# Both ends of a two-layer encoder trunk: constant products and VectorE scaling first, kept weight splits and shared squares last

## The chip, the cores and the metric

The kernel runs on one core of one Trainium2 chip. The core has five engines, each with its own instruction queue that is worked in order: TensorE (PE, matrix products; PEld is its weight load), VectorE (DVE), ScalarE (ACT), GpSimd (POOL) and SyncE (SP), which here issues most of the DMA transfers. The metric is the device time of one execution in microseconds (us); lower is better.

## The reference

The input is one sequence of 1024 frames with 1024 channels. Layer 0 mixes along time with RWKV-7 (a recurrence with data-dependent decay), layer 1 with a diagonal complex state-space model; each mixer is followed by a squared-ReLU MLP, and every sub-layer ends in a layer norm. All data are float32. Cut to what the change touches, the first low-rank projections and the last MLP with its norm:

```python
def layer_norm(x, g, b):
    mu = jnp.mean(x, axis=-1, keepdims=True)
    var = jnp.mean(jnp.square(x - mu), axis=-1, keepdims=True)
    return (x - mu) * lax.rsqrt(var + LN_EPS) * g + b

def rwkv7_time_mix(x, mu, w0, w1, w2, a0, a1, a2, g1, g2, ...):
    xx = jnp.pad(x, ((0, 0), (1, 0), (0, 0)))[:, :-1] - x
    xw = x + xx * mu[1]
    xa = x + xx * mu[4]
    w_pre = w0 + jnp.tanh(xw @ w1) @ w2
    a = jax.nn.sigmoid(a0 + (xa @ a1) @ a2)
    ...

def sq_relu_mlp(x, w1, w2):
    return jnp.square(jax.nn.relu(x @ w1)) @ w2

def reference(x, ...):
    h = x
    for i in range(2):
        mix = rwkv7_time_mix(h, ...) if i == 0 else s5_mix(h, ...)
        h = layer_norm(ALPHA * h + mix, ln_g[2 * i], ln_b[2 * i])
        h = layer_norm(ALPHA * h + sq_relu_mlp(h, mlp_w1[i], mlp_w2[i]),
                       ln_g[2 * i + 1], ln_b[2 * i + 1])
    return h
```

## The kernel before

Everything is held transposed: a tile has 128 channels as partitions and frames along the row, so a 1024-channel activation of half the sequence (512 frames, "A" or "B") is eight tiles of 128x512. Products are made at near float32 precision from two reduced-precision parts: `split` (L154) writes the high part with a cast on ACT (L155) and the low part, the remainder, with a subtraction on DVE (L156), and `mm3` (L206) sums three products (high by high, high by low, low by high), recorded at L204. Weights come by DMA into `wraw` (two buffers); the parts go to `whi` and `wlo` (three buffers each). A `wraw` buffer is free again when its subtraction on DVE is done.

**The beginning.** `rwkv_proj(0)` loads the eight tiles of x (`xs`, L272) and, with the first of them, two halves of the weight `wa1` (`first`, L274). `shifted` (L339) makes two products with the same weights, scaled once by 1 - mu and once by mu; `scaled` (L324) scales each 128x512 piece of weights on GpSimd (L331, two instructions of 128x4x64 where two coefficients share a piece), splits it and multiplies. The x tiles themselves are split to `oS`.

**The end.** The MLP of layer 1 for half B runs in blocks: `up(b)` (ub) makes two 128x512 tiles of squared ReLU (L1000 Relu, L1001 Square, then split into `qbuf`), `down(b)` (db) multiplies them by four weight tiles of 256 output channels and adds each product (six matmuls in one PSUM tile `d`, of which there are three) into the residual tiles `hB` on DVE (L1017). The last two `down` blocks, b = 2 and 3, are held back until all `up` blocks are done and are then run twice, once for each 256 frames (c = 0 and c = 1; L1525 to L1531). In both rounds each of the eight weight tiles is loaded and split (`wload`, L176): 16 loads. After c = 0 the generator `last_norm` (L917) of the first 256 frames is started at low priority (`rank(LN8R)`), so it lies beside the products of c = 1; its last part is resumed after the sums of the second norm, with `inorder` keeping its scaling (L958) behind the last of these sums (`last`).

**last_norm**, for 256 frames: the sums over the eight tiles go to GpSimd (L927, L928), DVE (L929, L930) and a product with a matrix of 1/1024 (`pm`, L934); DVE subtracts the mean (L937), ACT squares (L939 for k = 0 and 1, L942 with two `sq` buffers for the rest); six additions gather the squares into two tiles, two of them on GpSimd (k in LNT), four on DVE (L943); four matmuls with one column give the variance in rows (`pq`, L947); DVE adds epsilon (L949), GpSimd raises to -1/2 (L950), ACT spreads it (L952), PE transposes it back (`pr`, L955); DVE multiplies (L958), ACT applies gain and bias (L964; GpSimd for k = 6, L962), and each tile goes out by itself (L965, 128 KB, 8 stores for each c).

**The order.** The order within each engine isn't written by hand. A scheduler makes it when the program is built, from priorities (`rank`) and from a modelled timeline, over the whole program. The order at one place thus depends on what it takes everything before to last.

Of the kernel before, what the change touches and what calls it, by code (L numbers as in the profile page):

```python
# [32 lines left out]
TB = 2  # L33
JB = 4
# [28 lines left out]
LNU = (6,)  # L63
# [10 lines left out]
def trunk(ctx, tc, A):  # L74
# [183 lines left out]
    def rwkv_proj(H):  # L258
# [65 lines left out]
        def scaled(nm, parts):  # L324
            p = psd()
            n = 128 // len(parts)
            for k0 in range(0, KT, 4):
                w = first.pop(0) if first else wraw(nm, k0)
                for q, m in enumerate(parts):
                    wq = w[:, :, q * n : q * n + n]  # L330
                    G.tensor_mul(wq, wq, m[:, k0 : k0 + 4].unsqueeze(2).broadcast_to([128, 4, n]))  # L331
                hi = wp.tile([128, 4, 128], F32R, tag="whi", name="whi")
                lo = wp.tile([128, 4, 128], F32R, tag="wlo", name="wlo")
                split(w, hi, lo)
                for k in range(4):
                    mm3(p, hi[:, k], lo[:, k], xo[k0 + k][0], xo[k0 + k][1], k0 + k == 0, k0 + k == KT - 1)
            return p
# [580 lines left out]
    def last_norm(h, gi, c):  # L918
# [8 lines left out]
        G.tensor_add(a, hc[0], hc[1])  # L927
        G.tensor_add(a, a, hc[2])  # L928
# [6 lines left out]
        sab = tp.tile([128, 2, HW], F32, tag="la", name="sq01", bufs=2)  # L935
        for k, t in enumerate(hc):
            V.tensor_sub(t, t, pm)  # L937
            if k < 2:
                S.activation(sab[:, k], t, AF.Square)  # L939
            else:  # L940
                q = tp.tile([128, HT], F32, tag="m", name="sq")[:, 0:HW]
                S.activation(q, t, AF.Square)  # L942
                last = (G if k in LNT else V).tensor_add(sab[:, int(k in LNT)], sab[:, int(k in LNT)], q)  # L943
        pq = bank.tile([128, HT], F32, tag=tag, name="pq")
        for t in range(2):
            for j in range(2):
                PE.matmul(pq[:, t : t + 1], sab[:, j, t * 128 : (t + 1) * 128], ones_c[:, 0:1], start=j == 0, stop=j == 1)  # L947
        rs = tp.tile([128, 4], F32, tag="rs", name="rs")[:, 0:2]
        V.tensor_scalar(rs, pq[:, 0:2], LN_EPS, None, op0=ALU.add)  # L949
# [6 lines left out]
        after = (yield last) if c == 0 else None  # L956
        for k, t in enumerate(hc):
            scaled = V.tensor_mul(t, t, pr[:, 0:HW])  # L958
            if after:
                inorder([after, scaled])  # L960
            if k in LNU:
                G.tensor_scalar(t, t, vec(g, k), vec(b, k), op0=ALU.mult, op1=ALU.add)  # L962
            else:
                S.activation(t, t, AF.Identity, bias=vec(b, k), scale=vec(g, k))  # L964
            SP.dma_start(A["out"][k * 128 : (k + 1) * 128, HT + HW * c : HT + HW * c + HW], t)  # L965
        yield last
# [22 lines left out]
    def blocks(i, h, xo, qbuf):  # L989
# [16 lines left out]
        def down(b, first=False, cs=slice(0, HT)):  # L1006
            for n2 in range(C // nw):
                w = wload(A["mw2"][i, b, n2], KB2, nw)
                for n in range(nw // 128):
                    p = psd()[:, cs]  # L1010
                    dense(p, [(x[:, n * 128 : (n + 1) * 128], y[:, n * 128 : (n + 1) * 128]) for x, y in w],
                          [(x[:, cs], y[:, cs]) for x, y in qs[b]])
                    z = h[n2 * (nw // 128) + n][:, cs]
                    if first:
                        V.scalar_tensor_tensor(z, z, ALPHA, p, op0=ALU.mult, op1=ALU.add)
                    else:
                        V.tensor_add(z, z, p)  # L1017
# [505 lines left out]
    for b in range(JB - TB + 1, JB):  # L1523
        ub(b)
    for c in range(2):  # L1525
        for b in range(JB - TB, JB):
            db(b, False, slice(256 * c, 256 * c + 256))
# [78 lines left out]
```

## Time and profile before

| | us |
|---|---|
| median of three runs | 2608.95 (2604.10 to 2617.72) |
| the profiled execution | 2612.68 |
| its span, from the first to the last instruction | 2610.9 |
| PE busy | 2475.1 (95%) |
| DVE busy | 1814.7 (70%) |
| ACT busy | 1205.8 (46%) |
| POOL busy | 411.9 (16%) |

The page of the profile divides the span into 40 slices of 65 us. PE is busy for 0.7 of the first slice, 0.8 to 0.9 or more from there to the last, and 0.7 of the last. Busy times of PE are modelled, since matmuls overlap; the start of one matmul to the start of the next tells more than the length of one. In a timeline row the columns are: start, length of the group, engine, line, operation, result<-operands, count, and in brackets how long the engine had been idle and what ended it. In a group's row the numbers behind the bar are busy us and mean ns of one instruction.

### The profile page before, as it was taken

Reading aid. Unit: us, or ns where it says so; the run is one execution under the profiler, and the core shown is the slowest. Engines: PE = TensorE matmul, PEld = TensorE weight load, DVE = VectorE, ACT = ScalarE, POOL = GpSimd, SP = SyncE. Lnnn points to the kernel's source line nnn. Section 1 sums busy time; section 2 is a strip of 40 time slices with the busy share of each in tenths; the row PEclk is TensorE's granted clock in tenths of the full one; section 3 lists DMA queues with packets and bytes.
Section 4 is the critical chain, followed back from the end, with each engine's and each line's share of the span. In section 5 each row is a group of like instructions: output and inputs, shape, how many; then the busy total and the mean of one; then the engine's idle time right before and its main releaser. Section 6 shows DMA issues by size and latency. Waiting matters only on the chain.

```text
span 2610.9 us, 43753 instructions
## 1 busy us (share of the span) xinstructions
PE 2475.1 (95%) x16624; PEld 2008.2 (77%) x16624; DVE 1814.7 (70%) x3476; ACT 1205.8 (46%) x2155; POOL 411.9 (16%) x340
## 2 busy tenths in 40 slices
PE   7889989999889999999999999999999999999997
PEld 5778767788667788777778888887777888888876
DVE  7477676578887777999785555777587555555576
ACT  7555575455454443445534333434464333433344
POOL 3110431331221101011000000100212111111011
PEclk9989979899889999999999999999999999999998
DMA  4765455555222324446554323254222111111123
GB/s 150 256 200 179 160 185 183 172 181 167 89 71 80 100 85 122 150 133 168 171 198 168 97 94 96 89 190 138 90 85 77 57 47 51 56 50 53 49 96 114
DMA packets 206291, 319.68 MB, mean 122 GB/s; under 512 B 20097, under 2 KB 80641, under 8 KB 206081
## 3 DMA queue, kind: packets, MB, share of 16 engines
q1 hardware_dynamic: 204928, 314.79, 38.4%
q8 instruction: 131, 2.15, 0.3%
q10 hardware_dynamic: 1152, 2.10, 0.2%
q14 instruction: 80, 0.65, 0.1%
HBM read 252.85 MB, written 63.96 MB: 121 GB/s over the span
## 4 chain that ended last, share of the span: by engine, by line
PE 70%; DVE 13%; DMA 8%; ACT 4%; issue 3%; POOL 1%; SPq 1%; ACTq 0%; DVEq 0%; POOLq 0%
PE d L204 52%; PE d L1054 9%; DVE wlo L156 2%; DMA wraw<-in_mw_dram 2%; PE pA L614 1%; DMA ldsg<-s_sg 1%; ACT whi L155 1%; PE pU L732 1%; PE pR L722 1%; DVE oAl L156 1%; PE pO L743 1%; PE pO L741 1%; DVE KB L584 1%; PE pX L727 0%; DMA s_y<-yg 0%
## 5 line engine op out<-in xcount | busy, mean ns | idle before, releaser
L155 ACT CAST whi<-wraw 128x512 fp32r<-128x512 f32 x492 | 304.6, 620 | 634.6 <-PE d L204 438.6
L156 DVE TENSOR_TENSOR wlo<-wraw,whi 128x512 fp32r<-128x512 f32 x492 | 356.3, 724 | 242.3 <-ACT whi L155 236.7
L204 PE MATMUL d<-qbuf,whi 128*128 128x512 f32 (+1 forms) x1344 | 410.0, 389 | 8.1 <-DVE hA L1017 4.5
L204 PE MATMUL d<-oAh,whi 128*128 128x512 f32 (+1 forms) x768 | 311.0, 411 | 17.1 <-ACT ev L435 7.3
L204 PE MATMUL d<-oAh,wlo 128*128 128x512 f32 (+1 forms) x768 | 310.9, 407 | 9.8 <-DVE wlo L156 7.8
L204 PE MATMUL d<-oAl,whi 128*128 128x512 f32 (+1 forms) x768 | 310.9, 406 | 3.1 <-DVE oAl L156 3.1
L204 PEld LDWEIGHTS d<-qbuf,whi 128*128 128x128 f32 x1344 | 246.4, 190 | 63.5 <-DVE hA L1017 8.4
L204 PE MATMUL d<-qbuf,wlo 128*128 128x512 f32 (+1 forms) x672 | 256.6, 385 | 1.5 <-DVE wlo L156 1.4
L204 PE MATMUL d<-oBh,wlo 128*128 128x512 f32 x512 | 202.7, 396 | 3.6 <-DVE wlo L156 3.6
L204 PE MATMUL d<-oBh,whi 128*128 128x512 f32 x512 | 203.0, 397 | 3.0 <-ACT whi L155 2.6
L204 PE MATMUL d<-oBl,whi 128*128 128x512 f32 x512 | 200.7, 392 | 0.0
L204 PEld LDWEIGHTS d<-oAh,whi 128*128 128x128 f32 (+1 forms) x768 | 147.7, 194 | 53.9 <-ACT ev L435 9.6
L204 PEld LDWEIGHTS d<-oAh,wlo 128*128 128x128 f32 (+1 forms) x768 | 149.0, 194 | 44.8 <-DVE wlo L156 10.4
L204 PEld LDWEIGHTS d<-oAl,whi 128*128 128x128 f32 (+1 forms) x768 | 148.5, 194 | 34.7 <-DVE oAl L156 4.1
L204 PE MATMUL d<-qh,wlo 128*128 128x512 f32 x384 | 151.3, 394 | 0.0
L204 PE MATMUL d<-ql,whi 128*128 128x512 f32 x384 | 150.6, 392 | 0.0
L204 PEld LDWEIGHTS d<-qbuf,wlo 128*128 128x128 f32 x672 | 127.1, 190 | 28.7 <-DVE wlo L156 3.1
L204 PE MATMUL d<-qh,whi 128*128 128x512 f32 x384 | 149.2, 389 | 0.0
L1017 DVE TENSOR_TENSOR hB<-hB,d 128x512 f32<-128x512 f32 (+1 forms) x168 | 104.9, 633 | 34.2 <-PE d L204 32.3
L204 PEld LDWEIGHTS d<-oBh,wlo 128*128 128x128 f32 x512 | 96.5, 189 | 27.8 <-DVE wlo L156 5.3
L1017 DVE TENSOR_TENSOR hA<-hA,d 128x512 f32<-128x512 f32 x144 | 97.5, 681 | 27.3 <-PE d L204 26.0
L204 PEld LDWEIGHTS d<-oBh,whi 128*128 128x128 f32 x512 | 96.5, 189 | 24.8 <-ACT whi L155 3.2
(478 smaller groups left out, 5079.2 us busy)
## 6 DMA issues: line engine op xcount, KB each, us to landing
wraw<-in_mw_dram SPq DMA_DIRECT2D x376, 256.0 KB, 2.7
wraw<-in_glu_dram SPq DMA_DIRECT2D x64, 256.0 KB, 2.7
low<-wlo SPq DMA_DIRECT2D x52, 256.0 KB, 2.8
wlo<-low SPq DMA_DIRECT2D x52, 256.0 KB, 3.3
raw<-in_mw_dram SPq DMA_DIRECT2D x48, 256.0 KB, 2.6
wraw<-in_wk_dram SPq DMA_DIRECT2D x32, 256.0 KB, 3.4
wraw<-in_wr_dram SPq DMA_DIRECT2D x32, 256.0 KB, 3.9
wraw<-in_wv_dram SPq DMA_DIRECT2D x32, 256.0 KB, 4.2
```

The source lines that it names most:

```text
L155: S.copy(hi, src)
L156: (e or V).tensor_sub(lo, src, hi.bitcast(F32))
L204: bulk.append((PE.matmul(p, w, x, **kw).ins, x.shape[-1]))
L584: V.scalar_tensor_tensor(kb[hs, :, h], v3(a)[hs], 0.5, v3(cs)[hs], op0=ALU.mult, op1=ALU.mult)
L614: prods.append(PE.matmul(pp[h][:, cc, i], D.KB[j][hs, u].rearrange("p j l -> p (j l)"), D.AR[j][hs, u].rearrange("p j l -> p (j l)"), star ...
L722: hop.append(PE.matmul(pR[hs, i], at[:, h, c, i, 0], vsa[:, cl, h, i], start=True, stop=True))
L732: hop.append(PE.matmul(pU[hs, i], D.kbt[i // 2, c // 2][:, c % 2, i % 2, hs], vsa[:, cl, h, i], start=True, stop=True))
L741: PE.matmul(pO[bs, i], arc(i, 1)[hs], st[hs, i], start=i == 0, stop=False, skip_group_check=True)
L743: PE.matmul(pO[bs, i], at[:, h, c, i, 1], vsa[:, cl, h, i], start=False, stop=True, skip_group_check=True)
L1017: V.tensor_add(z, z, p)
L1054: PE.matmul(p, w[:, k], x, start=not add and k + j == 0, stop=k == 3 and j == 2, skip_group_check=True)
```

## The change

There are four edits.

1. **Beginning.** For the very first piece of `wa1` (`begin`), ten products of the identity with itself (`WARM`) are put ahead of the real products, into the same PSUM tile, which the first real product overwrites; and the scaling of that one piece is done by DVE and not by GpSimd.
2. **Kept weights.** In the last two `down` blocks, run for c = 0 and c = 1, the parts of the weights are written to `jp` buffers (tags t1 and t2, eight of each, last used by the blocks before) and kept: c = 0 loads and splits eight tiles, c = 1 loads none.
3. **The last norm.** All eight squares have buffers of their own. For c = 0 the sums of squares go as before. For c = 1 three additions on DVE remain (k = 5, 6, 7 onto 4), and five tiles go to `pq`, ten matmuls where there were four. For c = 1 the first two sums (`sab`) go to DVE in place of GpSimd. The scaling of c = 0 is now held back in two parts: k up to 2 behind the last sum of squares of c = 1, the rest behind its epsilon (`steps`). Gain and bias: for c = 0 GpSimd does k = 1, 4, 6 (was 6); for c = 1 DVE does k = 2, 5 (GpSimd did 6); ACT does the others.
4. **Stores** go out for two tiles at a time, from new `pair` buffers: 256 KB, four for each c.

```diff
@@ -31,6 +31,7 @@
 LNG = (1, 3, 5)
 LNT = (2, 5)
 TB = 2
+WARM = 10
 JB = 4
 TABB = 6
 LN8R = 400000
@@ -60,7 +61,7 @@
 STE = "scalar"
 MIX0R = 1500
 EVB = 4
-LNU = (6,)
+LNU = ((1, 4, 6), (2, 5))
 VM = ((0, 1, 3), (1, 3))
 DECAY = math.exp(-0.5)
 ALPHA = math.sqrt(2.0)
@@ -325,10 +326,14 @@
             p = psd()
             n = 128 // len(parts)
             for k0 in range(0, KT, 4):
+                begin = len(first) == 2
+                if begin:
+                    for _ in range(WARM):
+                        PE.matmul(p[:, 0:128], ident, ident, start=True, stop=True)
                 w = first.pop(0) if first else wraw(nm, k0)
                 for q, m in enumerate(parts):
                     wq = w[:, :, q * n : q * n + n]
-                    G.tensor_mul(wq, wq, m[:, k0 : k0 + 4].unsqueeze(2).broadcast_to([128, 4, n]))
+                    (V if begin else G).tensor_mul(wq, wq, m[:, k0 : k0 + 4].unsqueeze(2).broadcast_to([128, 4, n]))
                 hi = wp.tile([128, 4, 128], F32R, tag="whi", name="whi")
                 lo = wp.tile([128, 4, 128], F32R, tag="wlo", name="wlo")
                 split(w, hi, lo)
@@ -924,46 +929,59 @@
         hc = [t[:, cs] for t in h]
         ab = tp.tile([128, 2, HW], F32, tag="la", name="sab", bufs=2)
         a, b2 = ab[:, 0], ab[:, 1]
-        G.tensor_add(a, hc[0], hc[1])
-        G.tensor_add(a, a, hc[2])
+        E = V if c else G
+        E.tensor_add(a, hc[0], hc[1])
+        E.tensor_add(a, a, hc[2])
         V.tensor_add(b2, hc[3], hc[4])
         V.tensor_add(b2, b2, hc[5])
         pm = bank.tile([128, HT], F32, tag=tag, name="pm")[:, 0:HW]
         parts = [a, b2, hc[6], hc[7]]
         for k, x in enumerate(parts):
             PE.matmul(pm, ones_c, x, start=k == 0, stop=k == 3)
-        sab = tp.tile([128, 2, HW], F32, tag="la", name="sq01", bufs=2)
+        sq = []
         for k, t in enumerate(hc):
             V.tensor_sub(t, t, pm)
-            if k < 2:
-                S.activation(sab[:, k], t, AF.Square)
-            else:
-                q = tp.tile([128, HT], F32, tag="m", name="sq")[:, 0:HW]
-                S.activation(q, t, AF.Square)
-                last = (G if k in LNT else V).tensor_add(sab[:, int(k in LNT)], sab[:, int(k in LNT)], q)
+            if k % 2 == 0:
+                q = tp.tile([128, 2, HW], F32, tag=("la", "m", "ev", "ev")[k // 2], name="sq", bufs=(2, 2, EVB, EVB)[k // 2])
+            sq.append(q[:, k % 2])
+            S.activation(sq[k], t, AF.Square)
+        if c == 0:
+            for k in range(2, KT):
+                last = (G if k in LNT else V).tensor_add(sq[int(k in LNT)], sq[int(k in LNT)], sq[k])
+            parts = sq[0:2]
+        else:
+            for k in range(5, KT):
+                last = V.tensor_add(sq[4], sq[4], sq[k])
+            parts = sq[0:5]
         pq = bank.tile([128, HT], F32, tag=tag, name="pq")
-        for t in range(2):
-            for j in range(2):
-                PE.matmul(pq[:, t : t + 1], sab[:, j, t * 128 : (t + 1) * 128], ones_c[:, 0:1], start=j == 0, stop=j == 1)
+        for j, x in enumerate(parts):
+            for t in range(2):
+                PE.matmul(pq[:, t : t + 1], x[:, t * 128 : (t + 1) * 128], ones_c[:, 0:1],
+                          start=j + t == 0, stop=j == len(parts) - 1, skip_group_check=True)
         rs = tp.tile([128, 4], F32, tag="rs", name="rs")[:, 0:2]
-        V.tensor_scalar(rs, pq[:, 0:2], LN_EPS, None, op0=ALU.add)
+        steps = last, V.tensor_scalar(rs, pq[:, 0:2], LN_EPS, None, op0=ALU.add)
         G.tensor_tensor(rs, rs, mhalf[:, 0:2], op=ALU.pow)
         rb = tp.tile([128, 4, 128], F32, tag="la", name="rb", bufs=2)
         S.copy(rb[:, 0:2], rs.unsqueeze(2).broadcast_to([128, 2, 128]))
         pr = bank.tile([128, HT], F32, tag=tag, name="pr")
         for j in range(2):
             PE.transpose(pr[:, j * 128 : (j + 1) * 128], rb[:, j], ident)
-        after = (yield last) if c == 0 else None
+        after = (yield steps) if c == 0 else None
         for k, t in enumerate(hc):
+            if k % 2 == 0:
+                pair = jp.tile([128, 2, HW], F32, tag=("qh", "ql")[c], name="pair", bufs=6)
             scaled = V.tensor_mul(t, t, pr[:, 0:HW])
             if after:
-                inorder([after, scaled])
-            if k in LNU:
-                G.tensor_scalar(t, t, vec(g, k), vec(b, k), op0=ALU.mult, op1=ALU.add)
+                inorder([after[int(k > 2)], scaled])
+            y = pair[:, k % 2]
+            if k in LNU[c]:
+                (V if c else G).tensor_scalar(y, t, vec(g, k), vec(b, k), op0=ALU.mult, op1=ALU.add)
             else:
-                S.activation(t, t, AF.Identity, bias=vec(b, k), scale=vec(g, k))
-            SP.dma_start(A["out"][k * 128 : (k + 1) * 128, HT + HW * c : HT + HW * c + HW], t)
-        yield last
+                S.activation(y, t, AF.Identity, bias=vec(b, k), scale=vec(g, k))
+            if k % 2:
+                SP.dma_start(A["out"][k * 128 - 128 : k * 128 + 128, HT + HW * c : HT + HW * c + HW]
+                             .rearrange("(k p) t -> p k t", p=128), pair)
+        yield steps
 
     def yload(H):
         ys = []
@@ -1003,9 +1021,22 @@
                 split(r, qt[:, 0], qt[:, 1])
                 qs[b].append((qt[:, 0], qt[:, 1]))
 
-        def down(b, first=False, cs=slice(0, HT)):
+        def kept(src):
+            raw = wp.tile([128, KB2, nw], F32, tag="wraw", name="wraw", bufs=2)
+            SP.dma_start(raw, src)
+            hi, lo = (jp.tile([128, HT], F32R, tag=t, name="k" + t, bufs=8).rearrange("p (k n) -> p k n", k=KB2)
+                      for t in ("t1", "t2"))
+            split(raw, hi, lo)
+            return [(hi[:, k], lo[:, k]) for k in range(KB2)]
+
+        def down(b, first=False, cs=slice(0, HT), keep=None):
             for n2 in range(C // nw):
-                w = wload(A["mw2"][i, b, n2], KB2, nw)
+                if keep is None:
+                    w = wload(A["mw2"][i, b, n2], KB2, nw)
+                else:
+                    if (b, n2) not in keep:
+                        keep[b, n2] = kept(A["mw2"][i, b, n2])
+                    w = keep[b, n2]
                 for n in range(nw // 128):
                     p = psd()[:, cs]
                     dense(p, [(x[:, n * 128 : (n + 1) * 128], y[:, n * 128 : (n + 1) * 128]) for x, y in w],
@@ -1522,9 +1553,10 @@
         db(b)
     for b in range(JB - TB + 1, JB):
         ub(b)
+    keep = {}
     for c in range(2):
         for b in range(JB - TB, JB):
-            db(b, False, slice(256 * c, 256 * c + 256))
+            db(b, False, slice(256 * c, 256 * c + 256), keep)
         if c == 0:
             with rank(LN8R):
                 early = last_norm(hB, 3, 0)
```

What the scheduler makes of it, at three places. In the rows of the change the line numbers are its own: L156 and L157 are the cast and the subtraction of `split`, L1018 and L1019 the Relu and Square of `up`, L1048 the addition into hB, L943 the subtraction of the mean, L954 the sums of squares, L973 the scaling, L962 the epsilon, L980 and L978 gain and bias.

ACT, from the last weight tiles of the last `up` to the last weight tile of the rounds c. Before (whi are casts of weights, the last 16 of them those of c = 0 and c = 1; rl and qbuf are Relu, Square and cast of the last `up`):

```order
L155 CAST whi<-wraw 128x512 x4
L1000 ACTIVATE rl<-d 128x512
L1001 ACTIVATE rl<-rl 128x512
L155 CAST qbuf<-rl 128x512
L155 CAST whi<-wraw 128x512 x2
L1000 ACTIVATE rl<-d 128x512
L1001 ACTIVATE rl<-rl 128x512
L155 CAST whi<-wraw 128x512
L155 CAST qbuf<-rl 128x512
L155 CAST whi<-wraw 128x512 x7
```

Now (the kt with a number are the high parts of the eight kept tiles, in order):

```order
L156 CAST kt_24879<-wraw 128x512
L1018 ACTIVATE rl<-d 128x512
L156 CAST kt_24901<-wraw 128x512
L1019 ACTIVATE rl<-rl 128x512
L156 CAST kt_24923<-wraw 128x512
L156 CAST qbuf<-rl 128x512
L156 CAST kt_24945<-wraw 128x512
L156 CAST kt_24967<-wraw 128x512
L1018 ACTIVATE rl<-d 128x512
L1019 ACTIVATE rl<-rl 128x512
L156 CAST qbuf<-rl 128x512
L156 CAST kt_24989<-wraw 128x512
```

Before the second Relu stood three casts of the rounds c; now five do, and the fifth is of the first tile of block 3.

DVE, from the last additions into hB to the end. Before:

```order
L1017 TENSOR_TENSOR hB<-hB,d 128x256
L937 TENSOR_TENSOR hB<-hB,pm 128x256 x8
L943 TENSOR_TENSOR sq_25281<-sq_25281,sq 128x256 x4
L958 TENSOR_TENSOR hB<-hB,pr 128x256 x8
L949 TENSOR_SCALAR rs<-pq 128x2
L958 TENSOR_TENSOR hB<-hB,pr 128x256 x8
```

Now:

```order
L1048 TENSOR_TENSOR hB<-hB,d 128x256
L943 TENSOR_TENSOR hB<-hB,pm 128x256 x8
L954 TENSOR_TENSOR sq<-sq 128x256 x3
L973 TENSOR_TENSOR hB<-hB,pr 128x256 x3
L962 TENSOR_SCALAR rs<-pq 128x2
L973 TENSOR_TENSOR hB<-hB,pr 128x256 x13
L978 TENSOR_SCALAR pair<-hB,pv 128x256 x2
```

Five of the eight scalings of c = 0 moved from ahead of the epsilon (rs) of c = 1 to behind it.

SP, in the recurrence of layer 0, where projections for half B are stored (s_a, s_sg) beside loads for the recurrence (ldsg, lda, ldk) and weights (wlo, wraw). Before:

```order
L531 DMA ldsg<-s_sg 128x2x256
L531 DMA lda<-s_a 128x2x256
L394 DMA s_a<-ev 128x512
L394 DMA s_sg<-ev 128x512
L394 DMA s_a<-ev 128x512
L531 DMA ldk<-s_k 128x2x256
L184 DMA wlo<-low_2363 128x512
L394 DMA s_sg<-ev 128x512
```

Now:

```order
L536 DMA ldsg<-s_sg 128x2x256
L536 DMA lda<-s_a 128x2x256
L536 DMA ldk<-s_k 128x2x256
L399 DMA s_a<-ev 128x512
L399 DMA s_sg<-ev 128x512 x2
L806 DMA s_y<-gt 128x4x128
```

No edit touches this place: the load of ldk moved ahead of three stores. Such exchanges run through the recurrence on all five engines. From the middle of the state-space layer to the last blocks of the last MLP the order on PE is unchanged.

## The prediction

> **What bounds the kernel now.** I read the table of stretches first, then the timeline of both ends, then their groups. In a row of stretches stand the stretch, its length, the busy us of PE, PEld, DVE, ACT and POOL, the granted clock and DMA.
>
> ```profile
> 200.00:400.00 200.00, 180.77 (x1840) 148.03 (x1838) 150.28 (x352) 119.65 (x227) 63.14 (x56) 0.90 0.54 174
> 400.00:600.00 200.00, 183.75 (x1837) 153.46 (x1836) 131.86 (x338) 107.24 (x203) 54.39 (x44) 0.93 0.60 182
> 600.00:800.00 200.00, 178.31 (x1755) 145.88 (x1755) 169.98 (x380) 98.56 (x185) 53.20 (x43) 0.90 0.31 97
> 100.00:800.00 700.00, 632.86 (x5990) 519.58 (x5989) 519.53 (x1191) 377.12 (x706) 188.64 (x159) 0.91 0.51 160
> 800.00:2560.00 1760.00, 1727.77 (x10082) 1399.31 (x10081) 1197.41 (x2081) 740.03 (x1289) 188.35 (x137) 0.99 0.33 104
> 2591.40:2611.00 19.60, 4.42 (x20) 3.37 (x18) 10.45 (x31) 10.41 (x23) 3.23 (x5) 0.66 0.32 107
> ```
>
> From 800 to 2560 us PE is busy for 98%: nothing the change does can shorten that. It can win in the first 20 us, in the two rounds of the last blocks (2560 to 2591) and in the norm behind them (2591 to 2611), where PE is idle for 15 of 19.6 us. And the new order can win or lose in 100 to 800, where PE stands idle for 700 - 632.9 = 67 us.
>
> **Kept weights.** First the rounds c, of which the timeline shows the start, the pitch and the end:
>
> ```profile
> 2559.97 0.40 PE L204 MATMUL d<-qbuf,whi 128*128 128x256 f32 x2
> 2560.21 0.28 PE L204 MATMUL d<-qbuf,wlo 128*128 128x256 f32 x1
> 2560.56 0.29 PE L204 MATMUL d<-qbuf,wlo 128*128 128x256 f32 x1
> 2586.60 0.95 PE L947 MATMUL pq<-ones_c,sq 128*128 128x1 f32 x8
> 2587.41 0.48 PE L204 MATMUL d<-qbuf,whi 128*128 128x256 f32 x2
> 2591.37 1.03 PE L934 MATMUL pm<-sab,ones_c 128*128 128x256 f32 x4
> 2592.24 1.03 PE L934 MATMUL pm<-hB,ones_c 128*128 128x256 f32 x4
> ```
>
> Three products take 0.355 us (2560.21 to 2560.56), one 0.119. The 16 weight tiles of 12 products need 192 x 0.119 = 22.8 us. Between them stands the first norm: pm 1.7 (eight records at 0.87 for four, 2591.37 to 2592.24), pq 0.8 (2586.60 to 2587.41), pr some 0.2 (two records of half the columns of pm). That makes 25.5 us, yet the rounds last 2591.37 - 2559.97 = 31.4: PE idles for 5.9. The cause is the supply of weights:
>
> ```profile
> 2568.19 0.62 ACT L155 CAST whi<-wraw 128x512 fp32r<-128x512 f32 x1 [1.39 <-DVE hB L1017]
> 2570.34 0.63 ACT L155 CAST whi<-wraw 128x512 fp32r<-128x512 f32 x1 [1.53 <-DMA wraw<-in_mw_dram]
> 2574.50 0.62 ACT L155 CAST whi<-wraw 128x512 fp32r<-128x512 f32 x1 [1.50 <-DMA wraw<-in_mw_dram]
> 2571.72 2.69 DMA wraw<-in_mw_dram
> L156 DVE TENSOR_TENSOR wlo<-wraw,whi 128x512 fp32r<-128x512 f32 x14 | 9.7, 694 | 5.3 <-ACT whi L155 5.2
> ```
>
> A freed wraw buffer costs 2.78 us until its next cast starts (2571.72 to 2574.50), 0.62 of cast and 0.69 of subtraction: 4.1 us for two buffers, a tile each 2.05 us (the casts come 2.1 apart), where PE needs one each 12 x 0.119 = 1.43. With kept parts the second round loads nothing; that takes its part of the idle time away. The first round is still fed every 2.05 us, but its parts no longer wait for the three whi buffers, so it starts ahead:
>
> ```profile
> 2550.31 0.69 DVE L156 TENSOR_TENSOR wlo<-wraw,whi 128x512 fp32r<-128x512 f32 x1 [0.45 <-ACT whi L155]
> 2552.35 0.69 DVE L156 TENSOR_TENSOR wlo<-wraw,whi 128x512 fp32r<-128x512 f32 x1 [1.35 <-ACT whi L155]
> 2554.45 0.62 ACT L155 CAST whi<-wraw 128x512 fp32r<-128x512 f32 x1 [2.12 <-PE d L204]
> 2560.47 0.59 ACT L1000 ACTIVATE rl<-d 128x512 f32<-128x512 f32 x1
> ```
>
> Buffers come free at 2551.00 and 2553.04, so the kept casts fall at 2553.8 (2554.45 before, held by PE), 2555.8, 2557.9, 2559.9, **2562.0**, 2564.1 and so on. Here ACT's new order bites: the second Relu stands behind the fifth of these. It could start at 2560.47; now it ends near 2563.2, and until then it holds one of the three PSUM tiles d. PE has two products' worth (2559.97 to 2561.4), then stands for 1.8 us. DVE's subtractions of that tile and of the eighth stand ahead of additions that free d: 0.5 more. In the second round the eight subtractions of the mean (2.74 us, row below) hold up the additions, while three free d feed PE for 3 x 0.71 = 2.1: with the start of the addition behind them and its release some 1.3. Idle is then 3.6 in place of 5.9: **-2.3 us**. Ends: -5.9, if PE never waits; 0, if the first round eats all of it.
>
> **The norm at the end.** All times from S, the first subtraction of the mean:
>
> ```profile
> 2593.37 2.74 DVE L937 TENSOR_TENSOR hB<-hB,pm 128x256 f32<-128x256 f32 x8 [1.38 <-PE pm L934]
> 2593.89 0.72 ACT L939 ACTIVATE sq<-hB 128x256 f32<-128x256 f32 x2 [4.54 <-DVE hB L937]
> 2596.03 0.95 DVE L943 TENSOR_TENSOR sq<-sq,sq 128x256 f32<-128x256 f32 x2
> 2598.59 2.73 DVE L958 TENSOR_TENSOR hB<-hB,pr 128x256 f32<-128x256 f32 x8
> 2598.72 1.86 PE L947 MATMUL pq<-ones_c,sq 128*128 128x1 f32 x8 [5.46 <-DVE sq L943]
> 2601.24 0.15 DVE L949 TENSOR_SCALAR rs<-pq 128x2 f32<-128x2 f32 x1
> 2603.66 2.74 DVE L958 TENSOR_TENSOR hB<-hB,pr 128x256 f32<-128x256 f32 x8 [2.27 <-PE pr L955]
> 2604.11 3.55 ACT L964 ACTIVATE hB<-hB,pv 128x256 f32<-128x256 f32 x7 [1.24 <-DVE hB L958]
> 2608.17 0.41 SPq L965 DMA_DIRECT2D out_dram<-hB  x1
> out_dram<-hA ACTq DMA_DIRECT2D x8, 256.0 KB, 2.4
> out_dram<-hB SPq DMA_DIRECT2D x16, 128.0 KB, 1.9
> ```
>
> Before, squares wait for two shared buffers, the last sum ends just ahead of pq, at S+5.3, pq at S+7.2, and rs starts only at S+7.9, behind eight scalings of the other half (2598.59 + 2.73). The scaling of c = 1 starts at S+10.3, the last gain and bias ends at S+14.3.
>
> Now every square has its buffer: the last ends some 0.55 behind the subtractions, S+3.3. Three chained sums (0.5 apart, from the pair in 0.95) run from S+2.7 to S+4.2. Eight of the ten pq matmuls are done by then; two are left, four records at 1.86 / 8: S+5.1. DVE's three scalings (0.34 each) end at S+5.2, so rs starts there. From rs to the scaling took 2603.66 - 2601.24 = 2.4 us and takes some 0.2 more, since ACT has a gain and bias of c = 0 ahead of rb: S+7.8, 2.5 earlier. ACT then has six tiles where it had seven, 0.5 less, while DVE's two (k = 2, 5) end beside them. Stores: the last began 0.5 behind ACT's end, since sixteen issues queue on SP; with eight the queue is gone, but 256 KB land 0.5 later (2.4 against 1.9). Nothing either way. Sum **-3.0 us**; ends -4.0 (a faster pq and pr, no chain in the sums) and -1.5 (pair stores and DVE's share late).
>
> The sums of c = 1 that GpSimd did ended before they were needed. On DVE they are four additions between the last four into hB, 7 x 0.34 = 2.3 us against 3 x 0.71 = 2.1 us of products: within 0.2, left out.
>
> Row 2598.72 gives pq 1.86 us after 5.46 us of idle PE; the same work took 0.8 at 2586.60 between products. [...]
>
> **The beginning.** The ten constant products stand on PE ahead of work that waits for weights until 9.02 us:
>
> ```profile
> 9.02 1.22 PE L204 MATMUL d<-oS,whi 128*128 128x512 f32 x2 [9.02 <-ACT whi L155]
> PEld d L204 <- DVE oS L156: 4.8, 7, 1.5
> 6.28 2.05 POOL wsc L331 x2
> 6.14 0.69 DVE L156 TENSOR_TENSOR oS<-xs,oS 128x512 fp32r<-128x512 f32 x1 [2.31 <-ACT oS L155]
> 6.76 1.08 DVE L297 SCALAR_TENSOR_TENSOR m<-xs,pv,m 128x512 f32<-128x512 f32 x1
> 20.60 0.74 DVE L297 SCALAR_TENSOR_TENSOR m<-xs,pv,m 128x512 f32<-128x512 f32 x1
> ```
>
> They hide there, at 20 records of some 0.23 (the pq row) 4.7 us from 1.5 on, when the identity is there. They speed up products that wait for DVE's oS anyway (4.8 us in seven waits): 0. The scaling took GpSimd 2.05 us, to 8.33; DVE, free at 6.83, needs two instructions of 256 columns, 0.34 each (2.74 / 8 above), to 7.5. That is -0.8 for the first cast, but 0.7 us of work more on an engine that runs without a pause from 9 to 21 us. GpSimd scales the second piece in the meantime, and the mul-add at 6.76 beside it took 1.08; the one at 20.60, without it, took 0.74. I take **-0.3**; ends -2 (weights of the second product come 2 us earlier and all of it lasts) and +1.
>
> [...]
>
> **The order elsewhere.** The recurrence is reordered on all engines, with no work added. Its cost isn't in the trace. Three neighbouring stretches of 200 us, alike in work, differ by 3 to 5.4 us of PE time (183.75, 180.77, 178.31); over 700 us, with parts that cancel, I bound it at 7 us both ways and take 0.
>
> **Sum.** -2.3 - 3.0 - 0.3 = -5.6 us. The profiled execution lasted 2612.7 (span 2610.9 and 1.8 around it): 2607.1. The median of the three runs shown is 2608.95, 3.7 less; against it 2603.3, rounded to **2603**. A measurement of this kernel tells about 0.5%, 13 us, from no change.
>
> **Rivals.**
> - *The end is as good as its idle time* (chance 0.15): the Relu isn't late, PE never waits, all at its best end: -5.9 - 4.0 - 2 = -11.9, 2597. For it: casts may come sooner than 2562.0. Against: 2.05 us per tile has been steady.
> - *The kept weights do not do what they say* (0.12): the first round loses to Relu and d all that the second wins: -3.3, 2605.7.
> - *The new order wins* (0.13): 7 to 12 us in 100 to 800 on top of the forecast: 2591 to 2596.
> - *The new order loses* (0.10): loads for the recurrence stand behind other stores and weights on SP. DVE already waits 5.4 us at the longest for ldsg:
>
> ```profile
> DVE ldsg L564 <- DMA ldsg<-s_sg: 30.9, 12, 5.4
> ```
>
> Twelve waits, 2.6 us each. If twelve loads come one such wait later, 31 us are added, 2634; half of them make 15, 2619. From 5.6 it is slower than before, from 19 by over 0.5%.
> - *The forecast* (0.50): 2603, give or take 5.
>
> **Chances and range.** Faster by over 0.5% (below 2596): most of the new order's win and part of the first rival, 0.20. Slower by over 0.5% (above 2622): part of the new order's loss, 0.06. Within: 0.74. The range reaches down over most of the two winning cases, to 2593, and up by the 7 us of order and the +1, to 2612; that leaves some 0.1 out on each side.
>
> **What would show it.** Right: in the second round no load of wraw and products 0.119 apart but for one gap of 1 to 1.5 us behind the subtractions of the mean; in the first round a gap near 1.8 us that ends with the second Relu; from S to the last gain and bias 11 to 11.5 us in place of 14.3; stores of 256 KB, eight in all. Wrong: a first gap of nothing (the casts come sooner), or a PE time in 100 to 800 that has moved by over 7 us; then order and not the edits sets the sum.

## The result, and the profile after

| | us |
|---|---|
| before, median of eight runs | 2608.46 (2604.10 to 2617.72) |
| changed, median of eight runs | 2619.53 (2616.25 to 2621.91) |
| ratio, 95% interval | 1.0049 (1.0037 to 1.0061) |
| profiled execution of the changed kernel, its span | 2621.12, 2619.4 |

The changed kernel is some 11 us slower by the medians (12.8 by the ratio); the prediction had 2603, at most 2612. One marker divides the loss. The first product of the last MLP's `qh` blocks stands behind everything that the recurrence and the first MLP do, and ahead of everything that the edits at the end touch. In the timeline of TensorE (start, duration) it stands in the kernel before at

```profile
2029.93 0.40 PE L204 MATMUL d<-qh,whi 128*128 128x512 f32 x1
```

and in the changed kernel at

```profile
2042.33 0.40 PE L205 MATMUL d<-qh,whi 128*128 128x512 f32 x1
```

So 12.4 us are lost ahead of it and some 4 us are won behind it (2612.7 to 2621.1 is 8.4). The stretches of the changed kernel, with the columns of the prediction's table (length, busy us of PE, PEld, DVE, ACT, POOL, granted clock, DMA):

```profile
200.00:400.00 200.00, 175.68 (x1790) 145.03 (x1791) 148.16 (x357) 114.87 (x215) 59.45 (x54) 0.85 0.52 168
400.00:600.00 200.00, 183.52 (x1823) 147.69 (x1821) 139.28 (x317) 112.71 (x212) 58.81 (x47) 0.95 0.56 177
600.00:800.00 200.00, 178.85 (x1725) 146.83 (x1724) 160.15 (x380) 96.47 (x181) 44.18 (x37) 0.88 0.34 105
100.00:800.00 700.00, 626.45 (x5910) 510.20 (x5909) 514.73 (x1175) 376.79 (x702) 180.97 (x154) 0.90 0.50 159
800.00:2560.00 1760.00, 1727.12 (x10106) 1398.42 (x10105) 1203.66 (x2089) 740.25 (x1286) 199.39 (x142) 0.99 0.34 104
```

From 800 to 2560 us the busy time of PE has hardly changed (1727.12 us against 1727.77). From 100 to 800 PE executes 80 products fewer in the same time (5910 against 5990). The column to read is that of the counts: the busy time differs by 6.4 us only, since products took longer where the clock was at half: in the changed kernel one of 128x512 starts 0.43 us before the next at a granted clock of 0.50 (12.60 to 13.03 us) and 0.23 us at 1.00 (2570.05 to 2570.28).

The end, in TensorE's timeline (in brackets the idle time before, and what ended it):

```profile
2575.72 10.75 PE L205 MATMUL d<-qbuf,kt 128*128 128x256 f32 x78 [1.83 <-ACT rl L1018]
...
2594.24 4.37 PE L205 MATMUL d<-qbuf,kt 128*128 128x256 f32 x36 [1.11 <-DVE hB L1048]
...
2602.39 1.04 PE L940 MATMUL pm<-sab,ones_c 128*128 128x256 f32 x4
...
2605.31 1.95 PE L959 MATMUL pq<-ones_c,sq 128*128 128x1 f32 x16 [1.02 <-ACT sq L947]
2608.51 1.01 PE L959 MATMUL pq<-ones_c,sq 128*128 128x1 f32 x4 [1.25 <-DVE sq L954]
```

and in those of VectorE and ScalarE:

```profile
2604.33 2.74 DVE L943 TENSOR_TENSOR hB<-hB,pm 128x256 f32<-128x256 f32 x8 [1.32 <-PE pm L940]
...
2609.56 0.16 DVE L962 TENSOR_SCALAR rs<-pq 128x2 f32<-128x2 f32 x1
...
2611.75 2.74 DVE L973 TENSOR_TENSOR hB<-hB,pr 128x256 f32<-128x256 f32 x8 [0.39 <-PE pr L968]
```

```profile
2612.21 3.07 ACT L980 ACTIVATE pair<-hB,pv 128x256 f32<-128x256 f32 x6 [0.21 <-DVE hB L973]
```

The late Relu, the gap behind the subtractions and the steps of the norm are there as foretold; their numbers are set against the prediction's below.

### The profile page after: what moved, and what is told of

It reads as the page before. It is cut to its first block, busy times and chain, and to the rows that moved or that the text cites. A ratio compares the mean times of both kernels' runs of the same rounds, so it can differ in the third digit from the quotient of the medians.

```text
span 2619.4 us, 43735 instructions
## 1 busy us (share of the span) xinstructions
PE 2486.2 (95%) x16656; PEld 2015.8 (77%) x16656; DVE 1817.0 (69%) x3473; ACT 1203.5 (46%) x2144; POOL 410.4 (16%) x335
## 3 DMA queue, kind: packets, MB, share of 16 engines
q8 instruction: 131, 2.15, 0.3%
## 4 chain that ended last, share of the span: by engine, by line
PE 73%; DVE 13%; DMA 7%; ACT 4%; issue 2%; POOL 1%; SPq 0%; DVEq 0%; ACTq 0%; POOLq 0%
PE d L205 55%; PE d L1085 9%; DVE wlo L157 2%; PE pA L619 1%; DMA wraw<-in_mw_dram 1%; DMA ldsg<-s_sg 1%; DVE oAl L157 1%; PE pR L727 1%; DVE KB L588 1%; DVE KB L589 1%; DVE ldsg L569 1%; PE pU L737 1%; PE py L1420 1%; PE pk L1317 0%; DVE hA L1048 0%
## 5 line engine op out<-in xcount | busy, mean ns | idle before, releaser
L156 ACT CAST whi<-wraw 128x512 fp32r<-128x512 f32 x476 | 294.8, 620 | 616.1 <-PE d L205 419.2
L157 DVE TENSOR_TENSOR wlo<-wraw,whi 128x512 fp32r<-128x512 f32 x476 | 345.4, 726 | 238.6 <-ACT whi L156 230.6
L205 PE MATMUL d<-qbuf,whi 128*128 128x512 f32 x1216 | 385.6, 398 | 12.2 <-DVE hA L1048 8.8
L205 PEld LDWEIGHTS d<-qbuf,whi 128*128 128x128 f32 x1216 | 226.7, 190 | 66.1 <-DVE hA L1048 11.3
L205 PE MATMUL d<-qbuf,wlo 128*128 128x512 f32 x608 | 239.0, 395 | 0.0
L205 PEld LDWEIGHTS d<-qbuf,wlo 128*128 128x128 f32 x608 | 115.1, 189 | 25.6 <-DVE wlo L157 0.4
L1048 DVE TENSOR_TENSOR hB<-hB,d 128x512 f32<-128x512 f32 (+1 forms) x168 | 105.5, 633 | 36.8 <-PE d L205 35.0
L1048 DVE TENSOR_TENSOR hA<-hA,d 128x512 f32<-128x512 f32 x144 | 97.4, 681 | 23.5 <-PE d L205 22.0
```

The costliest lines, as they stand in the source:

```text
L156: S.copy(hi, src)
L157: (e or V).tensor_sub(lo, src, hi.bitcast(F32))
L205: bulk.append((PE.matmul(p, w, x, **kw).ins, x.shape[-1]))
```

## The experiments

Three theories at first. ORDER: the scheduler's new order of the recurrence costs some 14 us, and the end wins 3 to 4. CLOCK: the constant products disturb the clock. START: VectorE's scaling itself delays the beginning, and all that follows. On the chips used here the kernel before took 2600 to 2603 us, so each kernel is compared by its ratio to the kernel before on the same chip; 0.001 is 2.6 us.

**One part at a time.** *e1_endonly* is the changed kernel without the edits at the beginning:

```diff
-                if begin:
-                    for _ in range(WARM):
-                        PE.matmul(p[:, 0:128], ident, ident, start=True, stop=True)
...
-                    (V if begin else G).tensor_mul(wq, wq, m[:, k0 : k0 + 4].unsqueeze(2).broadcast_to([128, 4, n]))
+                    G.tensor_mul(wq, wq, m[:, k0 : k0 + 4].unsqueeze(2).broadcast_to([128, 4, n]))
```

> The kernel before with the edits of the end alone (kept weights, last norm, stores); GpSimd scales, no constant products. The order up to the last blocks of the last MLP is that of before on every engine. Theories for the 11 us by which the changed kernel is slower: ORDER (the recurrence in its new order costs some 14 us, the end wins some 3 to 4), CLOCK (the ten constant products disturb the granted clock), START (VectorE's scaling costs time by itself). All three expect -3 to -4 us here, since the two traces show the end 3.9 us shorter; the rival that the end's gain hangs on where the recurrence ends expects 0.

Measured: 0.9981 (0.9968 to 0.9993), -4.9 us. *e2_vscale* is the kernel before with VectorE's scaling alone, `(V if begin else G)`.

> The kernel before with VectorE's scaling of the first weight piece alone. The order of the recurrence is then that of the changed kernel. ORDER expects +12 to +16 us; START as much; CLOCK 0, within 2 us.

Measured: 1.0074 (1.0060 to 1.0087), +19 us. *e3_warm* is the kernel before with the ten constant products alone.

> The kernel before with the ten constant products alone. The order on all engines is that of before but for the added products. ORDER and START expect 0, within 2 us; CLOCK expects +12 to +16 us and a lower granted clock between 100 and 800 us.

Measured: 1.0014 (1.0001 to 1.0026), +3.6 us: more than nothing, but not the loss. So CLOCK falls, and moving one scaling to VectorE is what costs. *e4_null4* separates ORDER from START: it leaves the scaling on GpSimd, and sets the constant `cmask` four times more to the same ones, at the start.

```diff
     V.memset(cmask, 1.0)
+    V.memset(cmask, 1.0)
+    V.memset(cmask, 1.0)
+    V.memset(cmask, 1.0)
+    V.memset(cmask, 1.0)
```

> The kernel before with one 128x512 memset on VectorE written four more times at the start (2 us of VectorE while it waits for the first x tile). Nothing else is edited, yet the scheduler gives another order from the first projections through the recurrence. ORDER expects a time that differs from before by more than 4 us, of either sign, with the difference between 100 and 1330 us; CLOCK and START expect 0, within 2 us.

Measured: 1.0061 (1.0046 to 1.0076), +16 us, by four instructions of 0.48 us that no other engine waits for. (Not all of them lie where VectorE would wait: they start at 3.07, 4.41, 6.47 and 7.56 us, the last two among its first work.) They make VectorE's beginning longer for the scheduler, and with it the order of the recurrence another. Three more kernels with such fillings test whether it is the order or the 2 us.

> The kernel before with VectorE's scaling of the first product's weights and two more fillings of cmask (0.48 us each). Its order on all engines is that of e4_null4 but for the first few us, and e4_null4 has no scaling on VectorE. ORDER: as e4_null4, 1.006 of the kernel before, +10 to +18 us, within 4 us of it. START (the scaling itself costs): over 4 us more or less than e4_null4.

Measured: 1.0054 (1.0036 to 1.0071). Same order, and within the intervals the same loss (+14 us): a cost of the scaling itself doesn't show.

> The kernel before with one more filling of cmask (0.48 us of VectorE at the start, where it waits), which leaves the order of every engine as it was. ORDER: 0, give or take 2 us. Were e4_null4's +14 us the fillings' own work, each would cost some 3.5 us: +3.5.

Measured: 0.9997 (0.9985 to 1.0009). Same order as before, no loss.

> The kernel before with two more fillings of cmask: a third order of the recurrence. ORDER gives no sign, since the order is a draw: it differs from the kernel before by over 4 us one way or the other, and from e4_null4 as well. Work of its own: +7.

Measured: 1.0061 (1.0039 to 1.0083). A third order is slower too, and by as much as e4_null4: the expectation that it would differ from that one was wrong. All three new orders that were run lose 14 to 19 us.

**The old order, held.** If ORDER is right, the changed kernel with the old order is fast. The build notes for each engine the order in which the instructions of the kernel before stand (`ORDER`, a table of numbers), and ties each instruction to its neighbour:

```diff
+def pin(tc, nc):
...
+                tc.add_manual_dep(i, last.name, mybir.DependencyInfo(
+                    mybir.DependencyClass.NoSync, mybir.DependencyReason.DATA), reason="order")
+            last = i
```

Such a dependency is meant to fix only where an instruction stands in its engine's queue; that holding costs no time that shows is seen in the 0.9986 of e9_vpin below. *e9_vpin* does it to e2_vscale, *e10_apin* to the whole change.

> The kernel with VectorE's scaling alone (e2_vscale, 1.0074 of the kernel before), its order held to that of the kernel before on all five engines by dependencies between neighbours on an engine; only the two scalings stand on another engine. ORDER: within 2.5 us of the kernel before, 0.999 to 1.001. START: as e2_vscale, 1.006 to 1.009, +16 to +23 us.

Measured: 0.9986 (0.9973 to 1.0000), -3.6 us, a little below what ORDER expected and far from START.

> The whole change, its order held to that of the kernel before (up to the last blocks, whose order is the change's own). ORDER: the end's -4.6 us of e1_endonly with 0 to +2.5 of the constant products (e3_warm): -5 to -2, 0.998 to 0.9992. START or another cost of the beginning's edits: as the changed kernel, 1.004 to 1.006.

Measured: 0.9979 (0.9967 to 0.9991), -5.5 us. With this ORDER is shown: the same instructions are some 23 us apart by their order alone (1.0074 of e2_vscale against 0.9986 of e9_vpin), and the whole change in the old order beats the kernel before. Holding an order isn't what wins: e11_vfill and e16_h610 below are held too, to e2_vscale's order (e16_h610 up to 610 us), and lose as e2_vscale does.

**What the new order does to TensorE.** The same stretches of e9_vpin

```profile
300.00:400.00 100.00, 85.99 (x788) 64.49 (x787) 81.64 (x184) 70.08 (x132) 36.01 (x27) 0.88 0.60 193
400.00:550.00 150.00, 138.76 (x1425) 112.03 (x1424) 93.77 (x222) 83.46 (x159) 41.36 (x33) 0.94 0.55 175
550.00:620.00 70.00, 66.05 (x761) 60.99 (x760) 50.67 (x132) 35.30 (x65) 15.60 (x15) 0.93 0.64 198
```

and of e2_vscale

```profile
300.00:400.00 100.00, 76.92 (x723) 58.40 (x722) 74.98 (x175) 60.62 (x114) 33.39 (x25) 0.78 0.52 172
400.00:550.00 150.00, 142.30 (x1495) 110.37 (x1493) 94.71 (x220) 85.28 (x164) 35.97 (x31) 0.98 0.53 168
550.00:620.00 70.00, 62.76 (x562) 58.54 (x563) 53.90 (x128) 35.27 (x63) 23.05 (x18) 0.85 0.67 208
```

show where they part: in 300 to 400 PE stands idle for 23 us in place of 14 and its clock is 0.78 in place of 0.88; 400 to 550 is better; in 550 to 620 idle time (7.2 against 4.0) and clock (0.85 against 0.93) are worse again. Summed over the records of products and of the clock up to the first `qh` product (2035.6 against 2016.3, 19.3 us), 6.5 us are more idle time, 12.1 are products at half clock (an estimate: 136.4 us of busy time against 112.1, which count for half by the 0.43 and 0.23 us above), 0.7 is left. This division is of one execution each and doesn't hold for the order as such. Of the 12.1 us only 5.6 have come when e2_vscale has done the work that e9_vpin has done by 800 us; the other 6.6 come behind it (13.0 us against 6.4), where e6_null1 in the old order has 13.1 as well. And e16_h610 below, which loses as much, has 14.6 us more idle time and 4.5 of half clock against e9_vpin. At one place half clock and idle time lie together: from 378 to 396 us the granted clock of e2_vscale is 0.53. Its timeline there:

```profile
383.89 1.11 PE L796 MATMUL py<-ident,o 128*128 128x128 f32 x4 [5.94 <-POOL o L788]
386.67 1.12 PE L562 MATMUL pn<-ident,sq 128*128 128x128 f32 x4 [1.66 <-ACT sq L559]
...
392.36 0.63 PE L204 MATMUL d<-oAh,wlo 128*128 128x512 f32 x1
...
397.19 0.39 PE L204 MATMUL d<-oAl,whi 128*128 128x512 f32 x1
```

The four transposes `py` of a unit of the recurrence stand next in PE's queue, and it waits 5.9 us for GpSimd's `o`, with the projections of the sequence's second half (`d`) behind them; afterwards a product takes 0.63 us and not 0.39. In e9_vpin the same transposes stand among those projections, and nobody waits:

```profile
389.14 0.60 PE L796 MATMUL py<-ident,o 128*128 128x128 f32 x4
389.49 0.47 PE L204 MATMUL d<-oAl,whi 128*128 128x512 f32 x1
```

**Is it the half clock?** If so, constant products in those waits would bring the time back. *e11_vfill* is e2_vscale in its own order, *e12_endfill* is e8_endfix (below) in its own, each with such products ahead of waiting groups, into PSUM tiles that the groups then overwrite:

```diff
+    def fill(name, p):
+        k = calls[name] = calls.get(name, -1) + 1
+        for _ in range(FILL.get((name, k), 0)):
+            fillers.append(PE.matmul(p[:, 0:128], ident, ident, start=True, stop=True).ins.name)
```

> e2_vscale with its own order held, and 42 constant products of 128x128 set ahead of seven waiting groups of products (12 ahead of the transposes py that wait 5.9 us, 12 ahead of pb that waits 6.5, the others ahead of py, pn and pR). Nothing waits for them but these groups. If half a clock behind long waits carries the loss: 17.1 us at half clock with 9.3 of work, and 20.5 with 14.1, go at full clock, -4.6 and -7.0; the products behind the waits start up to 0.5 us late each: 5 to 11 us below e2_vscale, 1.003 to 1.0055 of the kernel before. If the waits themselves carry it: as e2_vscale or up to 2 us above, 1.0065 to 1.0085.

Measured: 1.0082 (1.0062 to 1.0101): nothing comes back. But the products took little of the half clock away. Up to the first `qh` product it costs 66.8 us here (an estimate as above) against 68.2 in e2_vscale, and the projections behind the filled `py` still start 0.43 us apart, up to 400 us:

```profile
398.42 0.63 PE L211 MATMUL d<-oAh,wlo 128*128 128x512 f32 x1
```

So e11_vfill shows that such fillings don't help, and not what half clock costs.

> e8_endfix with its own order held and 34 constant products ahead of nine waiting groups, most of them around its stretch of 23.9 us at half clock at 691 us (14.1 us of work in it). If half a clock carries time there too: 4 to 9 us below e8_endfix, 0.9943 to 0.9963 of the kernel before. If the chain of the recurrence between the engines sets the time there: as e8_endfix, 0.997 to 0.999.

Measured: 0.9973 (0.9956 to 0.9990), against 0.9978 (0.9963 to 0.9993) of e8_endfix: nothing is seen here either, though the interval reaches down to what half clock would give (0.9963). In this pair the trace tells more. e8_endfix, the stretch and its first and last group of products (the group ends a step of the recurrence):

```profile
690.00:714.00 24.00, 12.61 (x119) 11.21 (x120) 22.30 (x36) 8.15 (x16) 14.06 (x11) 0.53 0.19 61
```

```profile
688.79 0.66 PE L561 MATMUL pn<-ident,sq 128*128 128x128 f32 x4
...
715.93 0.69 PE L743 MATMUL pO<-vsa,AT 128*64 128x64 f32 x16
```

and e12_endfill:

```profile
690.00:714.00 24.00, 16.50 (x178) 14.35 (x177) 23.23 (x36) 9.84 (x19) 14.07 (x11) 0.78 0.19 61
```

```profile
693.14 0.66 PE L570 MATMUL pn<-ident,sq 128*128 128x128 f32 x4 [0.19 <-ACT sq L566]
...
719.89 0.69 PE L755 MATMUL pO<-vsa,AT 128*64 128x64 f32 x16
```

The clock rose from 0.53 to 0.78, and from `pn` to `pO` it takes 26.8 us where it took 27.1: VectorE is busy for 22 to 23 of 24 us here, and PE follows the chain. Half clock thus cost nothing here, where PE is busy for 12.61 of 24 us. What e11 and e12 don't exclude is half clock where projections follow densely.

**Where in the order.** Four hybrids of the same instructions (e2_vscale's) are held to the one order up to a cut and to the other behind it; the edit is another table in `pin`. LATE and EARLY are named in their expectations.

> VectorE's scaling alone; e2_vscale's order on all engines for what stands ahead of 368 us in its trace, the order of the kernel before for all the rest. EARLY (the loss lies in 370 to 405 us, where TensorE has the recurrence alone to do): 0 to +3 us, 1.000 to 1.001. LATE (it lies in 550 to 610): the same, 0 to +3. AHEAD (work that was put ahead of 368 us already costs it): +10 or more.

Measured: 1.0029 (1.0016 to 1.0042), +7.5 us: between all that was expected.

> The same with the cut at 405 us. EARLY: +8 us or more, from 1.003. LATE: 0 to +3, since what is lost by 405 us is made up by 550 in e2_vscale.

Measured: 1.0026 (1.0014 to 1.0039), +6.8 us. The stretch of the 5.9 us wait adds nothing to e13_h368: EARLY falls. LATE's 0 to +3 is missed as well.

> The other way round: the order of the kernel before up to 405 us, e2_vscale's order behind it. EARLY: half of e2_vscale's +18 or less, at most 1.0035. LATE: +9 us or more, from 1.0035 on.

Measured: 1.0059 (1.0043 to 1.0076), +15 us, as LATE has it.

> As e13_h368 with the cut at 610 us. EARLY and LATE: +9 to +18 us, 1.0035 to 1.007. TAIL (the loss lies behind 610 us, in the chain of the second half's units): 0 to +5, at most 1.002.

Measured: 1.0074 (1.0056 to 1.0092), +19 us, a little above what LATE expected and all of e2_vscale's loss: TAIL falls. Some 7 us thus come with the order ahead of 368 us, and 12 with that between 405 and 610. (They don't add up strictly: the second part alone, e15_r405, costs 15.) The recurrence runs in eight units, four for each half of the sequence, and each unit in two parts. In GpSimd's timeline the output `o` of the seventh part (the last but one of the sequence's first half) and of the ninth (the first of its second half) shows what the order does there. e9_vpin:

```profile
546.55 1.30 POOL L788 TENSOR_TENSOR o<-o,vt 128x512 f32<-128x512 f32 x1 [1.62 <-DVE o L787]
648.74 1.30 POOL L788 TENSOR_TENSOR o<-o,vt 128x512 f32<-128x512 f32 x1 [2.28 <-DVE o L787]
```

e2_vscale:

```profile
529.49 1.29 POOL L788 TENSOR_TENSOR o<-o,vt 128x512 f32<-128x512 f32 x1 [1.86 <-DVE o L787]
664.80 1.29 POOL L788 TENSOR_TENSOR o<-o,vt 128x512 f32<-128x512 f32 x1 [2.58 <-DVE o L787]
```

The first half runs 17 us ahead, and the second half starts 16 us late. In e14_h405, with the old order from 405 us on, both are 10 us late, as all else is (556.92 and 658.54); in e15_r405 and e16_h610 they are 19 and 15 us early, then 17 and 19 late. A likely reading is that e2_vscale's order puts the first half's recurrence ahead of the second half's projections, for which the second half's recurrence then waits. It isn't shown, and it isn't the whole of it. In e7_null2 the seventh part is not early (551.39 us, against 550.21 in e6_null1 in the old order on the same chip), and the ninth still comes 18 us late. And by the sixteenth and last part e2_vscale is only 8 us behind e9_vpin (1027.72 against 1019.98), e16_h610 20 (1039.76), while both lose as much in the end. Which pair of instructions decides it in 405 to 610 stays open: no kernel moved a single one.

**The late Relu.** *e8_endfix* is e1_endonly with the casts from the fifth of the eight kept tiles on behind the last block's second Relu:

```diff
-            split(raw, hi, lo)
+            cast = S.copy(hi, raw)
+            V.tensor_sub(lo, raw, hi.bitcast(F32))
+            if late:
+                inorder([relu[-1], cast])
```

> e1_endonly, and the casts of the fifth to the sixteenth kept weight tile are set behind the second Relu of the last block. The stall of 1.8 us of TensorE on that Relu should go: 1 to 1.8 us less than e1_endonly, -5.5 to -6.5 us against the kernel before, with nothing late in its place. If the supply of weights takes it back (the casts come later by as much), the same as e1_endonly, -4.6.

Measured: 0.9978 (0.9963 to 0.9993) against 0.9981 (0.9968 to 0.9993) of e1_endonly: the same. The stall on Relu (0.96 us in e1_endonly) is gone, and waits of 0.36, 0.17 and 0.25 us for VectorE's additions stand in its place. Ahead of these additions stand subtractions of kept weights, which wait for their casts (0.60 us ahead of the one at 2544.65 us): the supply of weights takes it back. From the first product of the rounds to the `pm` behind them it takes 27.97 us, against 28.23.

## Why the prediction was wrong, step by step

- **The order elsewhere** is the step that failed: "over 700 us, with parts that cancel, I bound it at 7 us both ways and take 0". The three stretches that this was read from (2.5 to 5.4 us apart, not 3 to 5.4) are of one order, and tell how unlike the work of the stretches is, not how much an order can lose. Measured: +14 to +19 us in three new orders out of three (e2; e4 and e5, which share one; e7), none with the old one held. It also was the largest item of the change that no row bounded, and so deserved the widest range. Nor was so little to be told from no change as "about 0.5%, 13 us": eight runs of each kernel gave an interval of 3 us to either side.
- **The new order loses** (chance 0.10) gave the right side and size (2619 to 2634) by a wrong mechanism. What VectorE waits for the loads of `ldsg` doesn't grow, it falls. Over the whole span it is 32.3 us before (30.9 of it in 100 to 800, the prediction's row), and in the changed kernel

```profile
DVE ldsg L569 <- DMA ldsg<-s_sg: 24.5, 14, 4.7
```

  (22.4 us in 100 to 800). The loss lies in what stands ahead of what on the engines; which exchange makes it is open.
- **The test named for it**, "a PE time in 100 to 800 that has moved by over 7 us", missed: it moved by 6.4, downwards, while 12.4 us were lost. Busy time was no measure of the work here, with the clock at 0.90 in place of 0.91; the count of products was (5910 against 5990).
- **Kept weights**: the two waits are as told, the sum is not. PE waits 1.83 us for Relu (1.8), 1.11 behind the subtractions of the mean (1.3). From the first product of the rounds to the `pm` behind them it takes 30.05 us (2572.34 to 2602.39) where it took 31.4: -1.35 in place of -2.3 in this execution, and -3.2 in e1_endonly (28.2). With the same edits at the end, e1_endonly waits 0.96 us for Relu, and its 78 products behind that take 9.80 us in place of 10.75: the term differs by 1.8 us between these two executions.
- **The norm**: from S = 2604.33, rs starts at S+5.2 (5.2), the scaling at S+7.4 (7.8), the last gain and bias ends at S+10.95 (11 to 11.5; 14.3 before). The stores were costed at nothing; from the end of that ScalarE work to the end of the span it takes 4.1 us where it took 3.2. That term was 0.9 short: -2.5 from S to the end, in place of -3.0.
- **The clock at the end**: the last four records of `pq` go at 0.25 us (row 2608.51), where the prediction took 0.23 from row 2598.72 of before; the sixteen ahead of them go at 0.12 (row 2605.31). The granted clock is 1.00 from 2605.0 to 2607.1 us and 0.50 from 2608.5 to 2609.6.
- **The beginning**: VectorE scales in 0.75 us and the first real product starts at 6.87 us, 2.15 earlier (the first two records take 0.74 us, where they took 1.22). How much of that stays is hardly clear of noise: in the old order the scaling measures 0.9986 (0.9973 to 1.0000), 0 to 7 us less, where -0.3 was forecast. The constant products were put at 0; e3_warm has 0.3 to 7 us. In the changed kernel they run at the head of

```profile
1.42 4.63 PE L332 MATMUL d<-ident 128*128 128x128 f32 x20 [1.42 <-POOL ident masks.py:199]
6.87 0.74 PE L205 MATMUL d<-oS,whi 128*128 128x512 f32 x2 [0.82 <-ACT whi L156]
...
10.05 0.63 PE L205 MATMUL d<-oS,wlo 128*128 128x512 f32 x1
...
16.44 0.40 PE L205 MATMUL d<-oS,wlo 128*128 128x512 f32 x1
```

  and the granted clock is 1.00 from 6.2 to 9.6 us and 0.50 from 9.6 to 16.4, while the products behind them come singly up to 12.0 us (0.22 to 0.69 us of idle time ahead of four of them). That this is e3's loss isn't shown.
- **The sum without the order** was right: -5.6 forecast, -5.5 (-8.6 to -2.3) measured in e10_apin, partly by luck, because errors cancel: the rounds and the stores won less than their terms, and the beginning's two edits measured 3.6 us each, one down and one up. The edits did what the views of the ends said; the order took it back three times over.

## What to carry to other kernels

Where a scheduler orders the program, an edit is two changes: its own work, and a new order of all that is scheduled behind it. Compare the two orders before judging the edit; where they differ far from the edit, measure the edit with the old order held, and a null edit that changes the order alone. Two instructions of 0.48 us that no other engine waited for were enough here for 16 us, and holding the old order by dependencies between neighbours made the same change a win of 5.5 us.

## What the runs showed of the hardware

Two things were not expected. In e2_vscale PE waits 1.98 us for a DMA. Its products of 128x256 then start 0.12 us apart (578.69 to 578.81), from 579.47 us on 0.21 apart (579.47 to 579.68), and 0.12 again from 590.39 on (to 590.51), with no idle time of over 0.3 us in between (though 2.8 us of it are products of one column, `pb`, with two products `pA` among them):

```profile
578.47 0.39 PE L204 MATMUL d<-wlo,oAh 128*128 128x256 f32 x1 [1.98 <-DMA wlo<-low]
...
579.68 0.42 PE L204 MATMUL d<-whi,oAh 128*128 128x256 f32 x1
...
590.39 0.28 PE L204 MATMUL d<-wlo,oAh 128*128 128x256 f32 x1
```

If the wait is the cause, which isn't shown, it cost its 2 us here and up to 5 us more in the products behind it (an estimate: half of the 10.7 us from 579.47 to 590.16), where PE sets the pace. It wasn't so behind each such wait: in e9_vpin PE waits 2.29 us for a DMA, up to 386.73 us, and the products of 128x512 behind it start 0.23 us apart (387.06 to 387.29, and still 397.57 to 397.80).

And the share of half clock wasn't fixed by the order. Up to the first `qh` product it cost (estimates as above) 54.5 to 64.6 us in six kernels with the old order on these chips (e1, e3, e6, e8, e9, e10) and 68.2 to 75.1 in four with a new one (e2, e4, e5, e7). But it cost 59.6 and 60.5 in e15_r405 and e16_h610, which lose 15 and 19 us; and in the first comparison, whose chip is not on record, the kernel before has 71.1 in the old order, and the changed one 75.9. What sets this share wasn't tried.
